# HGRN2 head sums of two levels: full-width weights in place of two half-width products

## The chip, the cores and the metric

The kernel runs on one core of a Trainium2 chip. The metric is the time of one execution on the device in microseconds; what is compared is the median over several runs. Names of engines in the profile: PE is TensorE's matmul side, PEld its weight loads, DVE is VectorE, ACT is ScalarE, POOL is GpSimd, SP is SyncE.

## The reference, cut to what matters

A decoder trunk of two layers over 512 tokens and 1024 features in float32. Each layer has a SwiGLU half step, a mixer of three groups of heads (a short convolution, HGRN2, forgetting attention) with one projection in front and one behind, and a second SwiGLU half step. The change lies in HGRN2, which has four heads of 64 features and works in chunks of 64 tokens:

```python
def step(state, inp):
    qb, kb, vb, lfb = inp
    bcum = jnp.cumsum(lfb, axis=-2)
    rel = bcum[..., :, None, :] - bcum[..., None, :, :]
    decay = jnp.where(causal, jnp.exp(jnp.where(causal, rel, 0.0)), 0.0)
    scores = jnp.einsum('bhtd,bhsd,bhtsd->bhts', qb, kb, decay)
    o = (jnp.einsum('bhts,bhsv->bhtv', scores, vb)
         + jnp.einsum('bhtd,bhdv->bhtv', qb * jnp.exp(bcum), state))
...
```

The score of a query t and a key s in a chunk is a sum over 64 features of q k and a decay that depends on both tokens and on the feature.

## The kernel before, in words

**The whole.** The tokens lie along the free axis (512 of them), features on the 128 partitions, eight groups of features. Weights come from DRAM in granules of 128x1024 (tile `st`), ACT casts each to a rounded high part (L480), DVE makes the rest as a low part (L486), both in tile `hl`. A dense product is three matmuls: high by high, high by low, low by high (L499, L505, L506; in some streams by the list of L603, whose order is held by hand: all of them follow one another on TensorE). A scheduler sets the order of the instructions of the other engines and of all that is not chained, from its own costs; the buffers rotate in pools.

**HGRN2** (`hgrn`, from L1588 on) is a generator run twice per layer, `pr` 0 and 1, each for two heads on 128 partitions; `mix` advances both in turn and steps the forgetting attention's projections (`fox_qkv`, L603's products) between. The scores of a chunk are split by levels. With the tokens of a chunk numbered from 0, level 0 is the diagonal, level 1 the pairs of neighbours (2n+1, 2n), level l the pairs whose highest differing bit is bit l-1; inside one block of a level the decay can be written with one reference token, so the scores become plain products. `LEVELS` groups them: (0, 1), (2, 3), (4, 5), (6).

For each level `operands` makes a tile `t` of 128 features by 512 tokens. For levels 2 to 6 it holds decayed keys and queries (DVE L1702, L1703, ACT's exponential in the helper at L377, DVE L1705), and `score` multiplies them, 64x64 weights by 32 moving columns (L1723). For levels 0 and 1 each query has one key only, so no product of matrices is needed: the tile holds already q k decay, feature by feature (DVE L1691 for level 0; ACT L377, DVE L1695 and L1696 for level 1). What is missing is the sum over each head's 64 features. `score` makes it with TensorE (L1713): the tile is the stationary operand, and the two moving columns are `heads2`, 128x2, which has ones where a partition belongs to the head. The result is one number for each token (on the partitions) and head (two columns), in a bank of tag `sc`.

One bank serves both `pr` and both levels. A column of that bank belongs to a head and a pair of chunks: chunk 2i lies on partitions 0 to 63, chunk 2i+1 on 64 to 127, in columns i and i+4 of the level's eight. `place` reads them (DVE): L1734 writes the diagonal of the score tile `A` for all eight columns, L1739 puts level 1 into it with a predicated copy. Both of layer 0's and layer 1's calls have the same form.

**Around L1713.** Ahead of it on TensorE stand the four transposes of `fox_decay` (L1840, weights 128x8), and behind it the next granule of `fox_qkv` (L603, 128x128 weights by 512 columns). L1842 and L1844 of `fox_decay` run on DVE between. ACT copies the projection out of its banks (L1901) and squares it (L1875), DVE sums the squares (L1876).

Of the kernel before, what the change touches and what calls it, by code (L numbers as in the profile page):

```python
# [28 lines left out]
P = 128  # L29
# [52 lines left out]
CH = 64  # L82
NCH = T // CH
# [168 lines left out]
class Trunk:  # L252
# [1335 lines left out]
    def hgrn(self, l, pr, hp, z, q, v, sg, og, S, kb, b, both):  # L1588
# [12 lines left out]
        def shared(key, *tags):  # L1601

            if key not in both:
                both[key] = [self.bank(tag) for tag in tags]
            return [b[:, pr * T // 2 : (pr + 1) * T // 2] for b in both[key]]
# [52 lines left out]
        for i in range(4):  # L1658
            for par, hh in ((0, 0), (1, 1), (0, 1), (1, 0)):
                r = slice(CH * par, CH * par + CH)  # L1660
# [47 lines left out]
        def score(lev, e, sb, at):  # L1708

            if lev < 2:  # L1710
                for c in range(NCH):
                    r = slice(CH * (c % 2), CH * (c % 2) + CH)
                    nc.tensor.matmul(  # L1713
                        sb[0][r, 8 * at + c // 2 : 8 * at + 8 : 4], e[:, c * CH : (c + 1) * CH],
                        self.heads2, start=True, stop=True,
                    )
                return
            for i in range(4):
                for hh, par in ((0, 0), (1, 1), (0, 1), (1, 0)):
                    r, c = slice(64 * hh, 64 * hh + 64), 2 * i + par  # L1720
                    keys = e[r, c * CH : (c + 1) * CH]
                    out = sb[hh][CH * par : CH * par + CH, P * at + 32 * i : P * at + 32 * i + 32]
                    nc.tensor.matmul(  # L1723
                        out.rearrange("p (n w) -> p n w", w=2**lev // 2), keys, sides(lev)(keys, 1),
                        start=True, stop=True,
                    )
# [25 lines left out]
        for g, levels in enumerate(LEVELS):  # L1752
            now, ready = ready, []
            later = list(LEVELS[g + 1]) if g + 1 < len(LEVELS) else []
            sb = shared(g, *(("pt", "sc")[g % 2 == 0],) * (2 if g else 1))
            for at, lev in enumerate(levels):
                score(lev, now[at], sb, at)
            yield
            for at, lev in enumerate(levels):
                if later:  # L1760
                    ready.append(operands(later.pop(0)))
                place(lev, sb, at)
            ready += [operands(lev) for lev in later]
            if g == 0:

                lk = own("lk", [P, 2 * NCH - 1, HD])
                S2, sx, qx = lk[:, : NCH - 1], lk[:, NCH - 1 : 3 * NCH // 2 - 1], lk[:, 3 * NCH // 2 - 1 :]
                nc.scalar.copy(S2, S[:, :, : NCH - 1].rearrange("p v c -> p c v"))
                q4 = qe.rearrange("p (i two t) -> p i two t", two=2, t=CH)
                nc.sync.dma_start(qx[:64, 1:], q4[64:, 1:, 0, :])  # L1770
                nc.sync.dma_start(qx[64:], q4[:64, :, 1, :])
                nc.sync.dma_start(sx[:64, 1:], S2[64:, 1::2])
                nc.sync.dma_start(sx[64:], S2[:64, ::2])
            yield
# [3 lines left out]
        for i in range(4):  # L1778
            for par, hh in ((0, 0), (1, 1), (0, 1), (1, 0)):
                r = slice(CH * par, CH * par + CH)  # L1780
# [5 lines left out]
        for c, own_rows in ((c, w) for c in range(1, NCH, 2) for w in (True, False)):  # L1786
            for c in (c, c + 1):
                if c == NCH:
                    continue
                par, i = c % 2, c // 2  # L1790
                hh = par if own_rows else 1 - par
                r = slice(CH * par, CH * par + CH)
# [24 lines left out]
        r, t = tmp(), tmp()  # L1817
# [417 lines left out]
```

## Time and profile before

| what | value |
|---|---|
| median of three runs | 1732.21 us |
| lowest of them | 1731.29 us |
| the profiled execution | 1730.99 us |
| its span, first to last instruction | 1729.2 us |
| instructions in the span | 32556 |
| granted TensorE clock, mean | 1.000 |
| L1713: records, all in two short stretches | 128 loads, 128 matmuls, from 388.7 and 1245.3 us |
| DMA, mean | 152 GB/s |

The page lists for each engine its busy time with its share of the span, then the chain of work that ended last. A timeline row reads: start, length, engine, line, operation, the tiles (written <- read, moving operand first), the shapes and a count; in 128*64 128x2 the weights have 128 rows and 64 columns, and two columns are streamed on 128 partitions. A merged row goes from the first start to the last end of its records. The length of a matmul record holds latency, so overlapping records are normal, and the pace is read from starts. PEld rows are the loads of weights.

### The profile page before, as it was taken

Reading aid. Unit: us, or ns where it says so; the run is one execution under the profiler, and the core shown is the slowest. Engines: PE = TensorE matmul, PEld = TensorE weight load, DVE = VectorE, ACT = ScalarE, POOL = GpSimd, SP = SyncE. Lnnn points to the kernel's source line nnn. Section 1 sums busy time; section 2 is a strip of 40 time slices with the busy share of each in tenths; the row PEclk is TensorE's granted clock in tenths of the full one; section 3 lists DMA queues with packets and bytes.
Section 4 is the critical chain, followed back from the end, with each engine's and each line's share of the span. In section 5 each row is a group of like instructions: output and inputs, shape, how many; then the busy total and the mean of one; then the engine's idle time right before and its main releaser. Section 6 shows DMA issues by size and latency. Waiting matters only on the chain.

```text
span 1729.2 us, 32556 instructions
## 1 busy us (share of the span) xinstructions
PE 1724.9 (100%) x13161; PEld 1623.3 (94%) x13161; DVE 1420.3 (82%) x1988; ACT 1009.4 (58%) x1406; POOL 176.2 (10%) x174
## 2 busy tenths in 40 slices
PE   9999999999999999999999999999999999999999
PEld 8999999888888999999989999998988889999998
DVE  7988787678888898888689887876888889788884
ACT  5565565465776565566446655555667765655651
POOL 0011120100000112012001111201000000120210
PEclk9999999999999999999999999999999999999999
DMA  7778784243543967878266787933435447678672
GB/s 218 185 149 194 185 178 111 72 128 87 151 129 98 241 149 157 206 163 171 86 193 168 178 180 178 191 87 80 116 96 146 127 126 203 159 150 228 144 161 97
DMA packets 249766, 262.28 MB, mean 152 GB/s; under 512 B 25816, under 2 KB 221152, under 8 KB 249616
## 3 DMA queue, kind: packets, MB, share of 16 engines
q1 hardware_dynamic: 197344, 192.02, 37.2%
q0 software_dynamic: 52256, 68.19, 24.4%
q8 instruction: 103, 1.69, 0.4%
q14 instruction: 47, 0.39, 0.1%
q10 hardware_dynamic: 16, 0.00, 0.0%
HBM read 226.15 MB, written 2.17 MB: 132 GB/s over the span
## 4 chain that ended last, share of the span: by engine, by line
PE 100%; DMA 0%; DVE 0%; issue 0%
PE mm L499 11%; PE mm L505 11%; PE mm L506 11%; PE mm L603 9%; PE pt L499 7%; PE pt L506 7%; PE pt L505 7%; PE sc L499 6%; PE sc L506 6%; PE sc L505 6%; PE po L505 3%; PE po L499 3%; PE po L506 3%; PE po L603 2%; PE sc L1974 1%; PE po L2040 1%
## 5 line engine op out<-in xcount | busy, mean ns | idle before, releaser
L1075 DVE TENSOR_TENSOR hl<-w,hl 128x1024 fp32r<-128x1024 f32 x279 | 341.4, 1224 | 97.6 <-ACT hl L1071 95.8
L1071 ACT CAST hl<-w 128x1024 fp32r<-128x1024 f32 x279 | 292.8, 1049 | 205.5 <-PE mm L506 50.3
L486 DVE TENSOR_TENSOR hl<-st,hl 128x1024 fp32r<-128x1024 f32 (+3 forms) x151 | 159.1, 1056 | 95.9 <-ACT hl L480 95.2
L480 ACT CAST hl<-st 128x1024 fp32r<-128x1024 f32 (+3 forms) x151 | 137.4, 913 | 155.5 <-PE po L506 37.0
L499 PE MATMUL mm<-xc,hl 128*128 128x256 f32 x698 | 191.5, 275 | 0.0
L505 PE MATMUL mm<-xc,hl 128*128 128x256 f32 x696 | 191.5, 275 | 0.0
L506 PE MATMUL mm<-xc,hl 128*128 128x256 f32 x696 | 191.4, 275 | 0.0
L499 PE MATMUL pt<-xc,hl 128*128 128x256 f32 x546 | 150.1, 275 | 0.0
L505 PE MATMUL pt<-xc,hl 128*128 128x256 f32 x544 | 149.7, 275 | 0.0
L506 PE MATMUL pt<-xc,hl 128*128 128x256 f32 x544 | 149.6, 275 | 0.0
L499 PEld LDWEIGHTS mm<-xc,hl 128*128 128x128 f32 x698 | 133.9, 192 | 0.1
L505 PEld LDWEIGHTS mm<-xc,hl 128*128 128x128 f32 x696 | 133.6, 192 | 0.0
L506 PEld LDWEIGHTS mm<-xc,hl 128*128 128x128 f32 x696 | 133.6, 192 | 0.0
L499 PE MATMUL sc<-xc,hl 128*128 128x256 f32 (+1 forms) x466 | 127.9, 275 | 0.0
L505 PE MATMUL sc<-xc,hl 128*128 128x256 f32 x464 | 127.7, 275 | 0.0
L506 PE MATMUL sc<-xc,hl 128*128 128x256 f32 x464 | 127.6, 275 | 0.0
L603 PE MATMUL mm<-hl,x 128*128 128x512 f32 x432 | 107.2, 383 | 0.0
L499 PEld LDWEIGHTS pt<-xc,hl 128*128 128x128 f32 x546 | 104.6, 192 | 0.3
L505 PEld LDWEIGHTS pt<-xc,hl 128*128 128x128 f32 x544 | 104.4, 192 | 0.3
L506 PEld LDWEIGHTS pt<-xc,hl 128*128 128x128 f32 x544 | 104.4, 192 | 0.0
L499 PE MATMUL mm<-x,hl 128*128 128x512 f32 x272 | 103.4, 381 | 0.0
L506 PE MATMUL mm<-x,hl 128*128 128x512 f32 x272 | 103.1, 379 | 0.0
(540 smaller groups left out, 5310.9 us busy)
## 6 DMA issues: line engine op xcount, KB each, us to landing
w<-in_ffn_w_in_dram SPq DMA_DIRECT2D x124, 512.0 KB, 6.0
w<-in_ffn_w_out_dram POOLq DMA_DIRECT2D x50, 512.0 KB, 9.5
w<-in_ffn_w_out_dram SPq DMA_DIRECT2D x49, 512.0 KB, 4.4
st<-in_ffn_w_out_dram SPq DMA_DIRECT2D x39, 512.0 KB, 3.6
st<-in_w_mix_in_dram SPq DMA_DIRECT2D x72, 256.0 KB, 3.1
st<-in_ffn_w_in_dram SPq DMA_DIRECT2D x71, 256.0 KB, 3.2
w<-in_ffn_w_in_dram POOLq DMA_DIRECT2D x29, 512.0 KB, 10.0
w<-S POOLq DMA_DIRECT2D x29, 512.0 KB, 5.1
```

The costliest lines, as they stand in the source:

```text
L480: a = nc.scalar.copy(hi, src[:, c : c + w])
L486: b = nc.vector.tensor_sub(lo, src[:, c : c + w], hi)
L499: i = nc.tensor.matmul(acc[:, c], ah, bh[:, c.start // 2 : c.stop // 2, :], start=first and c.start == 0, stop=False, skip_group_check=True,)
L505: nc.tensor.matmul(acc, ah, bl, start=False, stop=False, skip_group_check=True)
L506: i = nc.tensor.matmul(acc, al, bh, start=False, stop=last, skip_group_check=True)
L603: self.follow("p", self.nc.tensor.matmul(acc, *((w, woven(x)) if toks is None else (x[:, toks], woven(w))), start=k == 0 and id(acc) not i ...
L1071: A(nc.scalar.copy(hi, src))
L1075: return lambda: V(nc.vector.tensor_sub(lo, src, hi))
L1974: mm = lambda *a, **k: E(nc.tensor.matmul(*a, skip_group_check=True, **k))
L2040: E(nc.tensor.matmul(self.ob[:, o * P : (o + len(at)) * P], half[2][:, j, h].rearrange("p a d -> p (a d)"), turned_in(part[:, at[0] : at[- ...
```

## The change

It touches one loop of `score`, for levels 0 and 1:

```diff
         def score(lev, e, sb, at):
 
             if lev < 2:
-                for c in range(NCH):
-                    r = slice(CH * (c % 2), CH * (c % 2) + CH)
+                for i in range(4):
                     nc.tensor.matmul(
-                        sb[0][r, 8 * at + c // 2 : 8 * at + 8 : 4], e[:, c * CH : (c + 1) * CH],
+                        sb[0][:, 8 * at + i : 8 * at + 8 : 4], e[:, i * P : (i + 1) * P],
                         self.heads2, start=True, stop=True,
                     )
                 return
```

Before, each of the eight chunks has its own product: 64 columns of weights, which fill the lower or the upper half of TensorE's columns by the partitions of the output. Now two chunks, 2i and 2i+1, make one product with 128 columns of weights. The result lies where it lay. Lines behind the loop have numbers one lower.

On TensorE nothing changes places. The piece in layer 0 before, L1840's transposes, then the four tiles (level 0 and 1 of `pr` 0, level 0 and 1 of `pr` 1):

```order
L1840 MATMUL pt_4356<-ident,fl_4351 8x128 x4
L1713 MATMUL sc_4367<-heads_352,t_4303 64x2 x8
L1713 MATMUL sc_4367<-heads_352,t_4305 64x2 x8
L1713 MATMUL sc_4367<-heads_352,t_4314 64x2 x8
L1713 MATMUL sc_4367<-heads_352,t_4316 64x2 x8
L603 MATMUL mm_4167<-hl_4439,x_399_3670 128x512 x2
```

and now:

```order
L1839 MATMUL pt_4356<-ident,fl_4351 8x128 x4
L1712 MATMUL sc_4367<-heads_352,t_4303 128x2 x4
L1712 MATMUL sc_4367<-heads_352,t_4305 128x2 x4
L1712 MATMUL sc_4367<-heads_352,t_4314 128x2 x4
L1712 MATMUL sc_4367<-heads_352,t_4316 128x2 x4
L603 MATMUL mm_4167<-hl_4423,x_399_3670 128x512 x2
```

Four instructions per tile where eight were; the neighbours are the same (buffers named later have numbers 16 lower).

The scheduler changes places at three points behind it, in both layers alike. On ACT, among the exponentials of levels 2 and 3 (t_4406, now t_4390, is level 3 of `pr` 0) and the square of the projection (fs), before:

```order
L1901 COPY qk_4166<-mm_4167 128x2x4x64
L1901 COPY qk_4166<-mm_4168 128x2x4x64
L377 ACTIVATE t_4406<-t_4406 128x512
L1875 ACTIVATE fs_4496<-qk_4166 128x512
L377 ACTIVATE t_4418<-t_4418 128x512
```

and now:

```order
L1900 COPY qk_4166<-mm_4167 128x2x4x64
L1900 COPY qk_4166<-mm_4168 128x2x4x64
L1874 ACTIVATE fs_4480<-qk_4166 128x512
L377 ACTIVATE t_4390<-t_4390 128x512
L377 ACTIVATE t_4402<-t_4402 128x512
```

The square has moved ahead of one exponential. Further on in ACT's queue a cast of a granule (L480, hl_4814 before) has moved ahead of the exponential of level 6 of `pr` 0 (t_4752) in the same way, and DVE's queue follows it there; before:

```order
L1879 TENSOR_TENSOR fm_4470<-fm_4470,inv_452_3910 128x32
L1705 TENSOR_TENSOR t_4752<-t_4752,q_3709 128x8x32
L1703 TENSOR_TENSOR t_4761<-b_3706 128x8x32
L486 TENSOR_TENSOR hl_4814<-st_4812,hl_4814 128x1024
L721 SCALAR_TENSOR_TENSOR ft_4472<-fm_4470,ft_4472 128x32
```

and now:

```order
L1878 TENSOR_TENSOR fm_4454<-fm_4454,inv_452_3910 128x32
L1703 TENSOR_TENSOR t_4745<-b_3706 128x8x32
L486 TENSOR_TENSOR hl_4798<-st_4796,hl_4798 128x1024
L1705 TENSOR_TENSOR t_4736<-t_4736,q_3709 128x8x32
L721 SCALAR_TENSOR_TENSOR ft_4456<-fm_4454,ft_4456 128x32
```

The product with the queries (L1705) has gone behind the low part of the granule (L486). POOL and SP keep their order.

## The prediction

> **What bounds the kernel now.** I read the page first, then the waits of TensorE, then the timeline around the changed line, then the weight loads grouped by shape.
>
> ```profile
> PE 1724.9 (100%) x13161; PEld 1623.3 (94%) x13161; DVE 1420.3 (82%) x1988; ACT 1009.4 (58%) x1406; POOL 176.2 (10%) x174
> PEclk9999999999999999999999999999999999999999
> PE 100%; DMA 0%; DVE 0%; issue 0%
> ```
>
> The first row says that TensorE is busy for 1724.9 of 1729.2 us, the second that its granted clock never falls, the third that the chain that ended last is TensorE's own work from one end to the other. So what lengthens or shortens TensorE's queue moves the end, unless TensorE waits for somebody afterwards. The list of waits has nearly nothing of that kind:
>
> ```profile
> PE po L2157 <- PEq L2220: 0.8, 1, 0.8
> ...
> PEld pt L1723 <- issue: 1.3, 4, 0.3
> ...
> PEld sc L1713 <- DVE S L1673: 0.4, 2, 0.2
> ```
>
> The first is all that the matmul side waits for. The other two are small stops of the weight loads; the last stands right before the changed line, 0.2 us in each of the two layers. There is no later stall in which extra work on TensorE could vanish.
>
> **The place.** Timeline of TensorE in layer 0 (start, length, engine, line):
>
> ```profile
> 387.98 0.38 PE L603 MATMUL po<-hl,x 128*128 128x512 f32 x1
> 388.19 0.60 PE L1840 MATMUL pt<-ident,fl 128*8 128x128 f32 x4
> 388.72 2.03 PE L1713 MATMUL sc<-heads,t 128*64 128x2 f32 x64
> ...
> 395.97 3.62 PE L603 MATMUL mm<-hl,x 128*128 128x512 f32 x16
> ...
> 400.72 0.59 PE L603 MATMUL po<-hl,x 128*128 128x512 f32 x2
> 401.24 2.07 PE L1723 MATMUL pt<-t 64*64 64x32 f32 x128
> ```
>
> Two narrow windows of the same timeline show the last two records of L1840 and the first of L603 apart:
>
> ```profile
> 388.41 0.38 PE L1840 MATMUL pt<-ident,fl 128*8 128x128 f32 x2
> ```
>
> ```profile
> 390.69 0.48 PE L603 MATMUL mm<-hl,x 128*128 128x512 f32 x1
> ```
>
> L1713 has 32 products in the program's order and 64 records here, so each product runs as two records. What does the block cost now? A record's length holds a latency besides its streaming: one of L603 alone takes 0.38 us (387.98), the sixteen of 395.97 together 3.62, so they start (3.62 - 0.38) / 15 = 0.216 us apart. The transposes of L1840 start (0.60 - 0.38) / 2 = 0.11 apart; the last starts at 388.52 and has streamed at 388.63. L603 behind the block starts at 390.69, but its first record is 0.48 long where 0.38 is usual: it stood 0.10 for its weights, and streams from 390.79. The block occupies 390.79 - 388.63 = 2.16 us.
>
> Of that, 388.72 - 388.63 = 0.09 lies ahead of its first load. The list of waits blames DVE's scan L1673 for it, but the first product needs only L1691's tile, and that is long there:
>
> ```profile
> 384.14 0.69 DVE L1691 TENSOR_TENSOR t<-q,lk 128x512 f32<-128x512 f32 x1
> ```
>
> The same stop stands before L1723, where no DVE is named: the record pair at 400.72 ends at 401.31, its streaming 0.16 earlier (0.38 - 0.216), at 401.15, and L1723 starts at 401.24, 0.09 later. I read it as the price of going from full-width weights to narrower ones; the 0.10 of L603's long first record is the price of going back.
>
> **The change, part by part.** It takes out 32 of 64 records in each of the two layers, and makes each of the others a load of 128 columns instead of 64. The two moving columns per record stay. What sets the pace of such records is the load, not the two columns:
>
> ```profile
> 388.72 1.95 PEld L1713 LDWEIGHTS sc<-heads,t 128*64 128x64 f32 x64 [0.22 <-DVE S L1673]
> ```
>
> The 64 loads run in pairs, one for tokens 0 to 63 in the lower columns and one for 64 to 127 in the upper. With 0.138 for one load (below), (1.95 - 0.14) / 31 = 0.058 us per pair. 32 pairs are 1.87 us; with the two changes of width (0.09 and 0.10) and the last pair's rest that is the 2.16.
>
> How long does a record with 128 columns take? Before has no float32 product with two moving columns and 128 weight columns. The nearest rows, loads by shape (count, busy us, mean ns):
>
> ```profile
> L603 PEld LDWEIGHTS mm<-hl,x 128*128 128x128 f32 x184 | 34.1, 189 | 4.8
> ...
> L2015 PEld LDWEIGHTS pt<-ident,P 128*128 128x128 f32 x20 | 2.4, 141 | 0.4
> ...
> L1713 PEld LDWEIGHTS sc<-heads,t 128*64 128x64 f32 x64 | 1.9, 138 | 0.2 <-DVE S L1673 0.2
> ...
> L1840 PEld LDWEIGHTS pt<-ident,fl 128*8 128x8 f32 x4 | 0.3, 87 | 0.2
> ```
>
> Products with 128 columns load in 189 ns, with 64 in 138: 51 ns for 64 columns more. How closely loads of 128 columns can follow each other is seen where few columns stream behind each, in the attention scores of L1974:
>
> ```profile
> 456.71 0.19 PEld L1974 LDWEIGHTS sc<-S,S 128*128 128x128 f32 x1
> 456.82 0.19 PEld L1974 LDWEIGHTS sc<-q,q 66*128 66x128 f32 x1
> ...
> 457.16 0.19 PEld L499 LDWEIGHTS mm<-x,hl 128*128 128x128 f32 x1
> ```
>
> ```profile
> 456.74 0.30 PE L1974 MATMUL sc<-S,S 128*128 128x128 f32 x1
> ```
>
> The last row is the fifth load: four steps in 0.45 us, 0.1125 each, nearly twice the 0.058 of the pair. So the question of this change is whether the two 64-column loads of a pair truly run at once (then a full load costs twice a pair's time, and the old form was better) or share one path (then a full load costs what a pair does). A load that had no partner answers it:
>
> ```profile
> 431.68 0.14 PEld L1797 LDWEIGHTS pt<-lk 64*64 64x64 f32 x1
> 431.73 0.13 PEld L1797 LDWEIGHTS sc<-lk 64*64 64x64 f32 x1
> 431.77 0.13 PEld L1797 LDWEIGHTS pt<-qe,lk 64*64 64x64 f32 x1
> ```
>
> The middle one starts 0.05 after the one before it and 0.04 ahead of the next; it takes 0.13, and those that start four within 0.02 us take the same 0.13. Company costs a 64-column load nothing, so the pair runs at once, and I take 0.1125 per full record. The ends: 0.058 below (a full load like a pair), 0.189 above (each load stands alone).
>
> The Trainium skill, page "TensorE: Matmul & The Clock Gate", section "LDWEIGHTS (loading the stationary operand)", says that a load's time goes by its columns alone, columns over 1.2 in ns: 53 for 64 and 107 for 128. By that page the block would be 32 x 0.107 = 3.41 us, +1.25 a layer and +2.5 in all; the trace's 0.058 and 0.1125 are 5 ns above each of its figures, and I keep the trace's. Its page "TensorEngine Tiling (Array Packing)", section "Key Properties", says that separate tiles load weights in parallel, which speaks against this change; the lone load of 0.13 us agrees.
>
> The sum for one layer: the first load can now start while the last transpose streams, as full-width loads do elsewhere (at 456.82 L1974 loads the next weights while its product of 456.74 is in flight), so both changes of width go. The loads start at 388.52, the 33rd, L603's own, 32 x 0.1125 = 3.60 later, and L603 streams at 392.23 instead of 390.79: **+1.44 us**. Layer 1 has the same block to the hundredth:
>
> ```profile
> 1245.32 2.03 PE L1713 MATMUL sc<-heads,t 128*64 128x2 f32 x64
> 1247.29 3.72 PE L603 MATMUL mm<-hl,x 128*128 128x512 f32 x16
> ```
>
> Two layers are **+2.88 us**.
>
> What is queued behind. DVE's L1734 reads the bank of these products, and at worst it waits for the last of them. And the scheduler changed places at three points: on ACT a square L1875 goes ahead of one exponential L377, and a cast L480 ahead of another; on DVE a low part L486 ahead of one L1705.
>
> ```profile
> L1713 PE MATMUL sc<-heads,t x128: 197/198/219, 388.7 to 1247.2; 128*64 128x2 f32 x128
> ```
>
> ```profile
> 391.11 0.67 DVE L1734 TENSOR_TENSOR A<-same,sc 128x512 f32<-128x512 f32 x1
> ...
> 400.33 0.42 DVE L1705 TENSOR_TENSOR t<-t,q 128x256 f32<-128x256 f32 x1
> ```
>
> ```profile
> 394.64 0.63 ACT L1875 ACTIVATE fs<-qk 128x512 f32<-128x512 f32 x1
> ...
> 410.30 1.04 ACT L480 CAST hl<-st 128x1024 fp32r<-128x1024 f32 x1
> ```
>
> ```profile
> 426.36 1.13 PE L1723 MATMUL pt<-t 64*64 64x32 f32 x64
> ```
>
> The last product would be ready near 388.63 + 3.60 + 0.2 (one record's length) = 392.4, so DVE starts L1734 up to 1.3 late. Behind it on DVE stand the operands of levels 2 and 3; the last is made at 400.33 to 400.75, and TensorE reads it in the fourth quarter of L1723's 128 records, from about 401.24 + 1.5 = 402.74. That is 2.0 us of cover, and TensorE itself comes 1.44 later: cost nothing; without the cover 1.3 a layer. The moved square delays an exponential by 0.63, inside the same cover. The cast goes ahead of an operand of level 6, which TensorE reads at 426.36, some 13 us after: nothing, 1.04 if bare. No transfer is added or moved past another.
>
> So the profiled execution, 1730.99 us (span 1729.2), becomes 1733.9. The median of the runs shown is 1732.21, 1.2 above it; against the median I forecast **1735.1 us**, 0.17% slower. A measurement of this kernel can tell about 2% from no change, 34.6 us, so this counts as the same.
>
> **Rivals.**
>
> *The halves share one path (not slower).* For it: L2015's transposes load 128 float32 columns in 141 ns, hardly over the 138 of L1713's 64, so a full load of plain float32 need not take 189. Against: those are transposes, and the lone 64-column load would then have been shorter than the accompanied ones. It decides if the new records start 0.058 apart: 32 x 0.058 = 1.87 against 2.16, -0.29 a layer, 1731.6 us. Chance 0.13.
>
> *Loads that stand alone.* If the two-column products leave a load nothing to hide behind, each record costs its 189 ns: 6.05 us, +3.89 a layer, 1740.0. Against it: L1974's are as long and come every 112, L1713's are 138 long and come every 58. Chance 0.04.
>
> *DVE becomes late.* If L1734's wait shifts DVE by more than 2.0 + 1.44 us beyond what I count, TensorE stalls at L1723; with 2 us over that, 1739.1. For it speaks only that DVE is full in this stretch (start and end, length, then the busy time of each engine):
>
> ```profile
> 391.00:400.00 9.00, 9.00 (x43) 7.89 (x42) 9.00 (x18) 7.39 (x13) 0.00 (x0) 1.00 0.16 36
> 400.00:410.00 10.00, 10.00 (x166) 8.71 (x165) 10.00 (x28) 4.86 (x8) 0.52 (x1) 1.00 0.54 161
> ```
>
> Against it, nothing moves DVE by more than the 1.3 counted. Chance 0.03.
>
> *The changes of width stay.* The edit does less than it says if the 0.09 and 0.10 remain, because L1840's weights are 8 wide: 3.60 + 0.19 - 2.16 = 1.63 a layer, 1735.5. Against: L1840 itself follows L603 without such a stop (387.98 + 0.216 = 388.20, and it starts at 388.19). Chance 0.02.
>
> **How the numbers follow.** The forecast has 0.78, the rivals the rest. Its own spread is the offset between 1730.99 and the median plus some tenths for the pace, 1733.5 to 1736; downward I go to the sharing case with the profiled execution's base (1730.99 - 0.6, rounded to 1730.5), upward half way to the lone loads, 1737.5. No case comes near 2%: even at 0.48 us a record, the longest row quoted, 64 records are 31 us. So same 0.98, and 0.01 on each side for what I have not thought of.
>
> **What would show it.** In the profile after: 32 records per layer of 128x2 with 128 weight columns; loads about 190 ns long, 0.112 apart, the block 3.6 us; no stop before it and no 0.48 us record behind; DVE idle about 1.2 us before L1734 (L1733 then); no new wait at L1723. A block of 1.9 us, loads 0.058 apart, would prove me wrong on the path; a gain or loss over 10 us, on everything.

## The result, and the profile after

The change makes the kernel slower by 0.3%: 1737.41 us median of 8 runs (1735.42 to 1739.75) against 1731.58 before in the same comparison, ratio 1.0032 with a 95% interval of 1.0021 to 1.0043. That is 5.8 us, where 2.9 were forecast. The interval leaves out 1, so the loss is real, though it is far below the 2% at which a change counts. One of the eight runs before took 6409.91 us; the other seven lie between 1730.75 and 1732.76 with a median of 1731.30, and against that the change costs 6.1 us. The profiled execution took 1735.43 us with a span of 1733.7.

The eight times of the changed kernel stand in groups: 1735.42, 1735.43, 1735.55; 1737.37, 1737.45, 1737.51; 1738.99, 1739.75. The mean granted clock of these runs is 0.999 in the first group, 0.998 in the second, 0.998 and 0.997 in the last. All 66 runs of the kernel before that were made beside the experiments have 1.000, and their times still lie between 1730.65 and 1733.32, so one time alone does not tell what the clock did.

The first block of the changed profile is as forecast. Timeline of TensorE, then of its weight loads, in layer 0:

```profile
388.12 0.60 PE L1839 MATMUL pt<-ident,fl 128*8 128x128 f32 x4
388.55 3.63 PE L1712 MATMUL sc<-heads,t 128*128 128x2 f32 x32
392.04 3.70 PE L603 MATMUL mm<-hl,x 128*128 128x512 f32 x16
```

```profile
388.44 3.65 PEld L1712 LDWEIGHTS sc<-heads,t 128*128 128x128 f32 x32
```

```profile
L1712 PEld LDWEIGHTS sc<-heads,t x32: 190/192/192, 388.4 to 391.9; 128*128 128x128 f32 x32
```

32 loads of 192 ns start (3.65 - 0.192) / 31 = 0.1115 us apart. They begin under the last transpose, with no stop ahead. L603's first record, shown alone in a narrow window, is 0.46 long where 0.38 is usual, so it streams from 392.12. The four transposes start 0.11 apart from 388.12, so the last has streamed at 388.56, just as L1712's first record starts, at 388.55. The block takes 3.57 us instead of 2.16.

```profile
392.04 0.46 PE L603 MATMUL mm<-hl,x 128*128 128x512 f32 x1
```

DVE waits for the last product, as counted (the bracket is its idle time), and the product behind that, L1722, has no longer stops than L1723 had before: four of up to 0.3 us, as before, though the list now names DVE at them.

```profile
392.22 0.69 DVE L1733 TENSOR_TENSOR A<-same,sc 128x512 f32<-128x512 f32 x1 [1.20 <-PE sc L1712]
```

```profile
PEld pt L1722 <- DVE t L1705: 0.7, 2, 0.3
...
PEld pt L1722 <- DVE fm L1875: 0.7, 2, 0.3
```

The last L1705 ahead of L1722 ends at 402.47, 1.72 us later than before, where L1722 itself starts 1.34 later, at 402.58. So 0.4 us of the cover is used up, and no stop has grown.

```profile
402.01 0.46 DVE L1705 TENSOR_TENSOR t<-t,q 128x256 f32<-128x256 f32 x1
```

What was not forecast stands in layer 1, right behind the same block. The row of sixteen L603 records, 3.70 long in layer 0 and 3.72 in layer 1 before, is 5.39 long:

```profile
1246.54 3.63 PE L1712 MATMUL sc<-heads,t 128*128 128x2 f32 x32
1250.04 5.39 PE L603 MATMUL mm<-hl,x 128*128 128x512 f32 x16
```

Nothing waits there: PE is busy without a gap. The view by windows (start and end, length, busy time of PE, PEld, DVE, ACT, POOL, granted clock, DMA share, GB/s) shows what changed:

```profile
1246.50:1250.60 4.10, 4.10 (x37) 4.05 (x36) 2.87 (x6) 2.27 (x3) 0.00 (x0) 1.00 0.37 87
1250.60:1254.00 3.40, 3.40 (x10) 2.65 (x9) 3.12 (x8) 0.00 (x0) 0.00 (x0) 0.50 0.22 45
1254.00:1257.00 3.00, 3.00 (x16) 2.62 (x15) 0.71 (x2) 2.87 (x6) 0.00 (x0) 0.99 0.00 0
```

For 3.4 us after the block the granted clock is 0.50, and then full again. Half of 3.4 is 1.7, which is what the sixteen records lost (5.39 - 3.70 = 1.69). The profiled execution has one such event; its page's row of clock tenths shows none of it, since a slice of 43 us averages it away, and the mean clock of the whole core is what gives it away: the 0.001 that is missing from 1.000 is 1.7 us of 1733.7.

The trace also shows when the clock can change. In every kept trace the changes lie on a grid of 3.413 us that starts at another moment in each execution: here full clock begins at 4.76 us and the event at 1250.62, 365 such steps later, and the event lasts one step. Cut along this grid, the block of layer 0 (388.55 to 392.12) lies in two steps, 1.92 us in one and 1.65 in the other. Of the block of layer 1 (1246.54 to 1250.12), 2.91 us lie in the one step ahead of the event:

```profile
387.05:390.47 3.42, 3.42 (x28) 3.12 (x27) 3.39 (x6) 2.11 (x3) 0.00 (x0) 1.00 0.23 57
390.47:393.88 3.41, 3.41 (x25) 3.20 (x25) 2.21 (x6) 1.20 (x2) 0.00 (x0) 1.00 0.36 86
...
1247.21:1250.62 3.41, 3.41 (x30) 3.36 (x30) 2.22 (x5) 2.27 (x3) 0.00 (x0) 1.00 0.38 90
1250.62:1254.04 3.42, 3.42 (x10) 2.67 (x9) 3.10 (x8) 0.00 (x0) 0.00 (x0) 0.50 0.22 44
```

### The profile page after: what moved, and what is told of

It is laid out like the page before. It is cut to its first block, busy times and chain, and to the rows that moved or that the text cites. A ratio compares the mean times of both kernels' runs of the same rounds, so it can differ in the third digit from the quotient of the medians.

```text
span 1733.7 us, 32428 instructions
## 1 busy us (share of the span) xinstructions
PE 1729.2 (100%) x13097; PEld 1627.7 (94%) x13097; DVE 1419.9 (82%) x1988; ACT 1009.3 (58%) x1406; POOL 176.2 (10%) x174
## 3 DMA queue, kind: packets, MB, share of 16 engines
q8 instruction: 103, 1.69, 0.4%
## 4 chain that ended last, share of the span: by engine, by line
PE 100%; ACT 0%; DVE 0%; issue 0%
PE mm L499 11%; PE mm L505 11%; PE mm L506 11%; PE mm L603 9%; PE pt L506 7%; PE pt L505 7%; PE pt L499 7%; PE sc L506 6%; PE sc L505 6%; PE sc L499 6%; PE po L505 3%; PE po L506 3%; PE po L499 3%; PE po L603 2%; PE sc L1973 1%; PE po L2039 1%
## 5 line engine op out<-in xcount | busy, mean ns | idle before, releaser
L486 DVE TENSOR_TENSOR hl<-st,hl 128x1024 fp32r<-128x1024 f32 (+3 forms) x151 | 159.4, 1058 | 93.4 <-ACT hl L480 92.7
L480 ACT CAST hl<-st 128x1024 fp32r<-128x1024 f32 (+3 forms) x151 | 137.4, 913 | 153.9 <-PE po L506 35.9
L603 PE MATMUL mm<-hl,x 128*128 128x512 f32 x432 | 108.9, 388 | 0.0
```

The lines of the kernel that those rows point to most:

```text
L480: a = nc.scalar.copy(hi, src[:, c : c + w])
L486: b = nc.vector.tensor_sub(lo, src[:, c : c + w], hi)
L603: self.follow("p", self.nc.tensor.matmul(acc, *((w, woven(x)) if toks is None else (x[:, toks], woven(w))), start=k == 0 and id(acc) not i ...
```

## The experiments

Every run here was compared with runs of the kernel before on the same chip: e1 to e4 on one, e5 and e6 on a second, e7 and e8 on a third. On each of the three some kernels have a lowered clock and others have none.

Two theories for the extra. **A**: a stretch in which few columns stream through TensorE's array makes the chip halve the clock for one window of 3.4 us, though TensorE is never idle; the loads' price itself is as forecast. **B**: the wider weight loads themselves, or something that came with the new order, cost the extra.

### e1_wide32: more moving columns, the same loads

```diff
-self.heads2 = c.tile([P, 2], F32, tag="heads2", name="heads2")
+self.heads2 = c.tile([P, 32], F32, tag="heads2", name="heads2")
...
-sb[0][:, 8 * at + i : 8 * at + 8 : 4], e[:, i * P : (i + 1) * P],
+sb[0][:, P * at + 32 * i : P * at + 32 * i + 32], e[:, i * P : (i + 1) * P],
...
```

What is left out here is `place`, which reads the sums from their new columns.

> The changed kernel with 32 moving columns instead of 2 (heads2 widened with zeros, the sums are its first two columns, read from there by L1733's and L1738's successors). Loads are 128 columns as before, so the block should stay 32 records at 0.112 us. Theory A (the steps of 1.7 us over the predicted +2.9 come from the clock, halved for 3.4 us because a block of two-column products looks idle): 32 columns make TensorE's array busier, so the granted clock is 1.000 in all or nearly all runs and the median is 1731.6 + 2.9 = 1734.5, ratio 1.0016. Rival B (the clock or the extra time has to do with the 128-column loads themselves): the clock is 0.997 to 0.999 again and the median about 1737.

Measured: 1736.04 us (1734.02 to 1737.44, 8 runs) against 1731.13, ratio 1.0027 (1.0017 to 1.0037); the clock is below 1.000 in 7 of 8 runs, and the one run at 1.000 is the fastest, 1734.02. The clock that A expected at full did not come: 32 columns were too few, and this run alone tells nothing between A and B. Its profile has layer 0 at full clock and an event in layer 1, which here begins before the block has ended (4.03 instead of 3.66):

```profile
388.32 3.66 PE L1712 MATMUL sc<-heads,t 128*128 128x32 f32 x32
```

```profile
1246.28 4.03 PE L1712 MATMUL sc<-heads,t 128*128 128x32 f32 x32
1250.12 5.03 PE L603 MATMUL mm<-hl,x 128*128 128x512 f32 x16
```

### e6_stream128 and e8_stream64: the array kept streaming

```diff
-self.heads2 = c.tile([P, 2], F32, tag="heads2", name="heads2")
+self.heads2 = c.tile([P, P], F32, tag="heads2", name="heads2")
...
-    nc.vector.memset(self.heads2[64 * h : 64 * h + 64, h : h + 1], 1.0)
+    nc.vector.memset(self.heads2[64 * h : 64 * h + 64, h::2], 1.0)
...
-sb[0][:, 8 * at + i : 8 * at + 8 : 4], e[:, i * P : (i + 1) * P],
+sb[0][:, 8 * at + 2 * i : 8 * at + 2 * i + P], e[:, i * P : (i + 1) * P],
...
```

`place` is changed here too. e8 is the same with 64 columns.

> The changed kernel with 128 moving columns: heads2 repeated 64 times, each product writes its two sums and 126 further columns that the next product overwrites or nobody reads. L1974's 128-column products kept the pace of 0.112 a load, so the block stays 3.6 us and the work is the changed kernel's: 1731.1 + 2.9 = 1734.0. Theory A (the clock falls because little is streamed through the array for a window of 3.4 us; 32 columns, a quarter of the time, were not enough everywhere): the array streams nearly all the time, clock 1.000 in every run, median 1734.0, ratio 1.0016. Rival B (the weight loads, not the missing streaming, are what the clock answers to): clock 0.998 to 0.999 and 1736 to 1737.5.

> The changed kernel with 64 moving columns (heads2 repeated 32 times, what follows the two sums is overwritten or not read): the load sets the pace, 3.6 us a block, 1731.4 + 2.7 = 1734.1 at full clock. A 64-column float32 product streams for about 0.05 of the 0.112 us, half the time, between the quarter of 32 columns (clock fell in most runs) and nearly all of 128 columns (never). Theory A with a threshold on the streamed share below a half: clock 1.000, 1734.1; above a half: steps of 1.7 us in some runs, 1734 to 1737.

Measured: e6 1734.05 us (1733.39 to 1734.51, 11 runs) against 1731.4, ratio 1.0013 (1.0005 to 1.0022); e8 1733.98 (1733.5 to 1734.9, 11 runs) against 1731.31, ratio 1.0016 (1.0007 to 1.0025). All 22 runs have clock 1.000. The blocks are as long as the changed kernel's, e6's first:

```profile
388.74 3.74 PE L1712 MATMUL sc<-heads,t 128*128 128x128 f32 x32
392.23 3.70 PE L603 MATMUL mm<-hl,x 128*128 128x512 f32 x16
```

```profile
388.66 3.68 PE L1712 MATMUL sc<-heads,t 128*128 128x64 f32 x32
```

Same loads, same pace, up to 64 times the columns streamed: the extra falls from 5.8 us to +2.65 and +2.67, and the events are gone. The grid does not explain this away: the profiled executions have 3.04 us (e8) and 3.10 us (e6) of layer 1's block inside one step, more than the 2.91 that brought the event in the changed kernel. B falls. What is left is the price of the loads.

### e2_apart: the same products in two pieces

```diff
-for g in run + run:
-    next(g)
-for _ in range(n):
+for place, g in enumerate(run + run):
+    next(g)
+    if step == 1 and place == 0:
+        next(dense)
+for _ in range(n - (step == 1)):
     next(dense)
...
-nc.tensor.matmul(
+self.follow("p", nc.tensor.matmul(
...
```

> The changed kernel with the products of the two head pairs set apart: 16 records, then 12 dense matmuls of L603 (2.6 us), then the other 16, fixed in TensorE's order. Same loads, same cost of loads: +2.9 us over before. Theory A (the length of the quiet stretch decides, 3.6 us in one piece fill a window of 3.4): two pieces of 1.8 us leave the clock at 1.000; median 1734.5. Rival B (any 128-column block lowers the clock, or the extra comes from elsewhere): clock below 1.000 and about 1737. The spare: if 0.5 us comes on top, it is the wait of the score tiles on DVE, whose order changes.

Measured: 1733.87 us (1733.55 to 1734.72, 11 runs), ratio 1.0015 (1.0006 to 1.0023), clock 1.000 in all runs.

```profile
388.73 1.84 PE L1714 MATMUL sc<-heads,t 128*128 128x2 f32 x16
390.43 2.84 PE L603 MATMUL mm<-hl,x 128*128 128x512 f32 x12
393.10 1.84 PE L1714 MATMUL sc<-heads,t 128*128 128x2 f32 x16
```

The very products of the change, two columns each, with 2.6 us of dense work in their middle: no event. What counts is how much of the stretch lies in one piece. The price of the loads is +2.74 here.

### e3_half_twice: the old loads, twice as many

```diff
-for c in range(NCH):
+for c in (*range(NCH), *range(NCH)):
```

> The kernel before, with each of the half-width products of levels 0 and 1 made twice into the same place (same result): 128 loads of 64 columns per layer, a block of 64 pairs x 0.058 + 0.19 = 3.9 us. By the pace alone +1.87 us a layer, 1731.6 + 3.7 = 1735.3. Theory A (length of the quiet stretch, whatever the width): the clock falls as in the changed kernel, 0.997 to 0.999, and the median is 1737 to 1739. Rival B (the full-width loads lower the clock): clock 1.000, 1735.3.

Measured: 1738.59 us (1738.27 to 1740.84, 5 runs), ratio 1.0047 (1.0034 to 1.0061), clock 0.998 or 0.997 in all runs.

```profile
388.94 3.90 PE L1713 MATMUL sc<-heads,t 128*64 128x2 f32 x128
392.77 5.41 PE L603 MATMUL mm<-hl,x 128*128 128x512 f32 x16
...
398.88 0.38 PE L603 MATMUL mm<-hl,x 128*128 128x512 f32 x1
```

```profile
1249.05 3.90 PE L1713 MATMUL sc<-heads,t 128*64 128x2 f32 x128
1252.88 5.41 PE L603 MATMUL mm<-hl,x 128*128 128x512 f32 x16
```

Half-width loads, and both layers have the event, 5.41 instead of 3.72: full width is not what the clock answers to. The loads alone would have cost 1.87 a layer, 1734.9; two events of 1.7 more are 1738.3.

### e5_level0_full and e7_one_full: how long a stretch it takes

```diff
-for c in range(NCH):
-    r = slice(CH * (c % 2), CH * (c % 2) + CH)
+if lev == 0:
+    for i in range(4):
+        nc.tensor.matmul(
+            sb[0][:, 8 * at + i : 8 * at + 8 : 4], e[:, i * P : (i + 1) * P],
+            self.heads2, start=True, stop=True,
+        )
+    return
+for c in range(NCH):
+    r = slice(CH * (c % 2), CH * (c % 2) + CH)
```

e7 has `if lev == 0 and pr == 0:` there.

> Half of the change: level 0 in full-width products, level 1 in half-width ones as before. Per layer 16 loads of 0.112 and 16 pairs of 0.058, 2.7 us, and two more changes of width (0.09 and 0.10 each time), 3.1 us instead of 2.16: +0.94 a layer, 1731.1 + 1.9 = 1733.0 at full clock. Theory A with a threshold near a whole quiet window of 3.4 us: clock 1.000, 1733.0. Theory A with a threshold well below it: some runs one step of 1.7 us higher, median 1733 to 1735. If the changes of width cost nothing, 1732.2.

> A quarter of the change: of the four tiles of a layer only level 0 of the first head pair in full-width products, the others half-width. Per layer 8 loads of 0.112 and 24 pairs of 0.058 and one change of width each way, 2.5 us: +0.33 a layer, 1731.4 + 0.7 = 1732.1 at full clock. The question is where the clock's threshold lies between the 2.2 us of before (never in the runs so far) and the 3.1 us of half the change (most runs): if it is a quiet share near half of a 3.4 us window or less, some runs have clock 0.999 and stand 1.7 us higher; if it is nearer three quarters or more, clock 1.000 in all and 1732.1.

Measured: e5 1735.18 us (1733.13 to 1737.13, 11 runs), ratio 1.0021 (1.0012 to 1.003), clock below 1.000 in 10 of 11 runs, and the one at 1.000 is the fastest, 1733.13. e7 1732.06 us (1731.13 to 1733.83, 11 runs), ratio 1.0006 (0.9998 to 1.0015), so not told from before; the four slowest of its runs (1733.36 to 1733.83) have clock 0.999, the other seven 1.000. e5's first block, with its widths in turn, and the event behind it:

```profile
389.08 0.95 PE L1713 MATMUL sc<-heads,t 128*128 128x2 f32 x8
389.97 0.64 PE L1720 MATMUL sc<-heads,t 128*64 128x2 f32 x16
390.53 1.05 PE L1713 MATMUL sc<-heads,t 128*128 128x2 f32 x8
391.51 0.63 PE L1720 MATMUL sc<-heads,t 128*64 128x2 f32 x16
392.08 5.41 PE L603 MATMUL mm<-hl,x 128*128 128x512 f32 x16
```

From 389.08 to 392.18 (L603's first record stands 0.10) are 3.10 us, the forecast sum with two changes of width each way. e7's block is 2.48 us by the same reading, 388.60 to 391.08:

```profile
388.60 0.95 PE L1713 MATMUL sc<-heads,t 128*128 128x2 f32 x8
389.48 1.57 PE L1720 MATMUL sc<-heads,t 128*64 128x2 f32 x48
390.98 2.86 PE L603 MATMUL mm<-hl,x 128*128 128x512 f32 x12
```

Put in order, with the length of the stretch in each layer:

| kernel | stretch, us | moving columns | runs with clock below 1.000 | median, us |
|---|---|---|---|---|
| e4 (below) | 1.65 | 2 | 0 of 11 | 1730.26 |
| e2 | 1.8 and 1.8, apart | 2 | 0 of 11 | 1733.87 |
| before | 2.16 | 2 | 0 of 66 | 1731.1 to 1731.4 |
| e7 | 2.48 | 2 | 4 of 11 | 1732.06 |
| e5 | 3.10 | 2 | 10 of 11 | 1735.18 |
| changed | 3.57 | 2 | 8 of 8 | 1737.41 |
| e3 | 4.0 | 2 | 5 of 5 | 1738.59 |
| e1 | 3.6 | 32 | 7 of 8 | 1736.04 |
| e8 | 3.6 | 64 | 0 of 11 | 1733.98 |
| e6 | 3.6 | 128 | 0 of 11 | 1734.05 |

The 66 runs of before are those beside the three groups of experiments (24, 21 and 21). The kernel before stood just under the length at which the clock begins to answer: in its profile both blocks lie whole in one step of the grid, 2.16 us, and the clock stays. The first one:

```profile
387.86:391.27 3.41, 3.41 (x74) 2.92 (x73) 3.38 (x7) 2.39 (x4) 0.00 (x0) 1.00 0.27 65
```

The steps of the profiled executions that hold most of a block, with the part of the block that lies in each and the clock of the step behind it:

| kernel, layer | step | part of the block in it, us | columns | clock behind it |
|---|---|---|---|---|
| changed, 0 | 387.05 to 390.47 | 1.92 | 2 | 1.00 |
| e5, 1 | 1249.67 to 1253.08 | 2.04 | 2 | 1.00 |
| before, 0 | 387.86 to 391.27 | 2.16 | 2 | 1.00 |
| e3, 1 | 1250.50 to 1253.91 | 2.48 | 2 | 0.50 |
| e3, 0 | 390.34 to 393.75 | 2.53 | 2 | 0.50 |
| e5, 0 | 389.51 to 392.92 | 2.67 | 2 | 0.50 |
| changed, 1 | 1247.21 to 1250.62 | 2.91 | 2 | 0.50 |
| e1, 0 | 389.24 to 392.65 | 2.65 | 32 | 1.00 |
| e1, 1 | 1245.98 to 1249.40 | 3.12 | 32 | 0.50 |
| e8, 1 | 1247.19 to 1250.60 | 3.04 | 64 | 1.00 |
| e6, 1 | 1247.18 to 1250.59 | 3.10 | 128 | 1.00 |

So the bound for two columns lies between 2.16 and 2.48 us inside one step of 3.41, and it is higher for 32 columns. An estimate puts these together: L1840's 128 columns stream for 0.11 us, so 32 columns fill about a quarter and 64 about half of a record's 0.112. The time without streaming is then 2.0 and 2.3 us in e1's two steps and 1.5 in e8's, and one bound between 2.16 and 2.3 us fits every row.

### e4_quarter: the other direction

```diff
-for c in range(NCH):
-    r = slice(CH * (c % 2), CH * (c % 2) + CH)
+for c in range(2 * NCH):
+    r = slice(32 * (c % 4), 32 * (c % 4) + 32)
...
-sb[0][r, 8 * at + c // 2 : 8 * at + 8 : 4], e[:, c * CH : (c + 1) * CH],
+sb[0][r, 8 * at + c // 4 : 8 * at + 8 : 4], e[:, 32 * c : 32 * c + 32],
```

> The kernel before with the other direction of the change: 32 tokens a product in a quarter of TensorE's columns, four at once, 128 records a layer. If a load's pace goes by its own columns and neighbours cost nothing (0.112 for 128, 0.058 for 64), a set of four costs about 0.031 us, 32 sets 1.0 us instead of 1.87, so -0.87 a layer and 1729.9 us in all, ratio 0.999, clock 1.000. Rival: a record has a floor near 0.0155 us (L1723's 128 records take 2.0 us), so 128 records take 2.0 us and the time is 1731.6 to 1731.9.

Measured: 1730.26 us (1729.64 to 1730.98, 11 runs) against 1731.13 (1730.75 to 1732.44, 24 runs), ratio 0.9994 (0.9986 to 1.0003): the lowest median of all kernels here, though the interval still holds 1.

```profile
388.41 1.53 PE L1713 MATMUL sc<-heads,t 128*32 128x2 f32 x128
```

```profile
388.41 1.33 PEld L1713 LDWEIGHTS sc<-heads,t 128*32 128x32 f32 x128 [0.22 <-DVE S L1673]
```

The 128 loads, each 0.11 long, take 1.33 us, (1.33 - 0.11) / 127 = 0.0096 apart, 0.038 for a set of four: neither the 0.031 of pure width nor the rival's floor of 0.0155 for each. With L603's 0.10 the stretch is 1.65 us, 0.51 less a layer than before, where 0.87 was expected. So the block is shorter, as the rule of width has it, but by less than the rule gives; what the rest of the 0.038 is, no run shows.

## Why the prediction was off by half, step by step

*Pairs run at once, a full load costs twice a pair.* Right. Forecast 0.1125 a load, measured 0.1115. The rival that the halves share one path gave 0.058 and is out; loads that stand alone (0.189) are out as well. The lone 0.13 us load in the trace of before pointed the right way, but it starts while the load of 431.68 (0.14 long) still runs, so it was less alone than the working says. What decides is the 0.1115.

*The sum of the block.* Right in mechanism and nearly in size: +1.44 a layer forecast, 3.57 - 2.16 = +1.41 in the profile, +2.65, +2.67 and +2.74 in the three kernels that keep the clock, against +2.88. The changes of width went, as forecast. One sign failed, that no 0.48 us record would stand behind the block: L603's first is 0.46 long. That is its own load, which the sum had as the 33rd, so it costs nothing more.

*What is queued behind.* Right: DVE stood 1.20 us where at most 1.3 were counted, no stop at L1722 is longer, and the +2.65 to +2.74 leave no room for a cost of the three places that the scheduler changed. The last operand came 1.72 us late where 1.3 were counted, inside the cover.

*"Its granted clock never falls."* This is the step that failed. I read the row of clock tenths as a property of the chip in this kernel and made every term of the sum at full clock; it was a property of the kernel's rhythm. The missing term: one event costs 1.7 us. A mean clock of 0.998 over 1736 us is about 6.9 us at half clock, two events, and 0.999 is one. By their clocks, three of the eight runs had one event and four had two; the last, at 0.997, would have three. The median lies among the runs with two: 2.7 for the loads and 2 x 1.7 are 6.1, as measured against 1731.30.

The base was off too, the other way. The 1732.21 under the forecast is the median of three runs of which one is the 6409.91; the 24, 21 and 21 runs of before made later have medians of 1731.13 to 1731.40. From there the same sum gives about 1734.2, so the high base hid 0.9 us of the miss. That the time still fell inside the stated range, by 0.1 us, is luck of that base and of a bound drawn for another reason, the loads that stand alone.

The Trainium skill's page "TensorE: Matmul & The Clock Gate", section "Part 1: The HAM clock gate (the "warmup" mystery)", has the two clocks and the window: half rate after at least one idle window of about 3.4 us. The trace agrees on the half (0.50) and on the length (3.4 us, 1.69 lost). It differs on the condition, if idle is read as a gap: here TensorE's row has no gap at all, and 2.48 us of two-column products within a step were enough; the measurement decides.

That the profiled execution had the event in one layer and not in the other follows from the grid: 2.91 us of the block lay in one step in layer 1, at most 1.92 in layer 0.

Left open: the run of 1738.99 has the clock of two events but stands 1.5 us above the other runs with two, and the runs with 0.997 (1739.75, and two of e3 above 1740) have room for a third event where there are two blocks; none of these has a trace. The bound between 2.16 and 2.3 us is worked out from the few profiled executions alone, and whether the clock answers to the columns streamed or to something that goes with them was not separated. Why a set of four quarter-width loads takes 0.038 and not 0.031 was not tried.

## What to carry to other kernels

When few columns stream behind each weight load, the load sets the pace, and narrow loads in separate column groups run at once: splitting 128 columns into two halves took 2.16 us where one full product took 3.57, and quarters 1.65. A row of full clock in a profile holds for that rhythm only: before stretching a phase in which the array streams little, compare its length with the 2.2 us that were harmless here. If it must be longer, dense work in its middle (2.6 us here) or more columns behind each load (64 here) kept the clock. A mean clock of 0.999 is the sign of such events, since times alone scatter by as much; the view by windows finds them.

## What the runs showed of the hardware that was not expected

- The clock fell to 0.50 for 3.4 us with TensorE busy without a gap, after 2.48 us or more of products with 2 moving columns (4 of 11 runs at 2.48, 10 of 11 at 3.10, all 13 at 3.57 and 4.0), and after 3.6 us with 32 columns (7 of 8), never with 64 or 128 (0 of 22).
- The clock changes on a grid of 3.413 us whose start differs from execution to execution (365 steps from 4.76 to 1250.62 in the changed kernel, 114 from 3.80 to 392.92 in e5). What decides is the part of the stretch within one step: 2.16 us with 2 columns brought no event, 2.48 did.
- A full-width float32 product with 2, 32, 64 or 128 moving columns takes the same 0.112 us a record (32 loads in 3.65 us in all four kernels); the columns are free up to there.
- Quarter-width loads start 0.0096 us apart on average, four of them 0.038, less than the pair of half-width loads (0.058).
